# Sums of later tokens kept in float32 ahead of the up projection, products and transposes in a fixed order on TensorE, and a tile of its own for C11

## The chip, the cores and the metric

The kernel runs on one core of a Trainium2 chip. The metric is the device time of one execution in microseconds, given as the median of several runs. The engines are named as in the profile: PE is TensorE's matmul, DVE is VectorE, ACT is ScalarE, POOL is GpSimd, and SP is SyncE, whose queue issues nearly all transfers.

## The reference

The reference is one layer of a hybrid decoder over 1024 tokens of width 1024. The change touches only the end of it, from the output projection of the merged mixers to the feed-forward part:

```python
x = x + merged @ w_out[l]
u = rms_norm(x, norm_mlp_g[l]) @ mlp_up[l]          # 1024 x 1024 @ 1024 x 4096
x = x + jnp.square(jax.nn.relu(u)) @ mlp_down[l]    # 1024 x 4096 @ 4096 x 1024
```

All arrays are float32.

## The kernel before

The whole kernel is written with a tile framework. Each engine runs its instructions in a fixed order, and a tile waits for the last readers of the buffer that it takes over. A buffer is named by a tag in a pool: two tiles with one tag share the buffer in turn. The order on each engine is set when the program is built, by a scheduler that takes the instructions in the order of the program and moves those forward that are ready. `tc.issue_after(ins)` pins the instructions that are written in its block behind `ins` on their engine.

Every float32 product is made of three matmuls of a split operand (`mm3`, lines 229 to 236): high by high (L233), high by low (L234), low by high (L235). The split of an operand is two instructions (`split`, lines 1364 to 1367): a cast on ACT (L1365, the high part) and a subtraction on POOL or DVE (L1366, the low part). Split weights stand in three buffers for high parts (`whi`) and three for low parts (`wlo`).

The last part of the kernel is the function `tail` (line 1279). It works in these stages:

- **The output projection**, for the first 512 tokens (hf 0) and then for the later 512 (hf 1), each in two halves of the columns (n). It accumulates in four PSUM banks at a time, adds the residual on DVE (L1358) and normalises each tile of 128 tokens (`norm_tile`, L1314; its last instruction is L1319 on DVE). For n = 1 the banks are two of tag `g` and two of tag `w`. The transposes of the normalised tiles (`transposed`, tiles `nt_f`) also use the two banks of tag `w`.
- **The operands of the up projection.** `mlp_up` is multiplied in 8 groups of 512 columns. Each group is a 2 by 2 block product in Winograd's form with seven products. The activations are split by features and tokens into B11 and B21 (first tokens, features below and above 512), B12 and B22 (later tokens). The seven operands are B11, B21, B22, and T1 = B12 - B11, T2 = B22 - T1, T3 = B12 - B22, T4 = B21 - T2. `first_half` makes B11 and B21 between matmuls of the output projection. `second_half(j)`, for j from 0 to 3, makes slice j of the other operands: it transposes slice j and slice 4 + j of the later tokens into two banks (`p12`, `p22`), forms the sums with scale and subtraction on DVE (L1476, L1477, L1479), and at once splits each of them into its high and low part. The sums live in a tile `tt` that alternates between the buffers of tags `l4` and `l5`.
- **The groups.** `up_a(g)` makes the products with B11 (bank tile `ux`, called X) and B21 (bank tile `uy`), copies X into the group's block C11 (L1400 on ACT), adds Y to it (L1413) and squares its positive part (L1418). `up_b(g)` makes the other five products with T2, T1, T3, B22 and T4, of which T2, T3 and T4 accumulate on top of X, forms the remaining blocks and sums of them, and stores seven blocks to DRAM for the down projection. The first products of groups 0 and 1 are placed between the calls of `second_half`.

All outputs of a group lie in three tiles `uo` of tags `l4`, `l5` and `r1`. C11 is the first half of the tile of tag `l4`, and the copy into it is written in the function `outputs` (lines 1396 to 1400). So the copy for group g + 1 has to wait until group g is done with the whole tile of tag `l4`. T2's product accumulates on X, so it has to wait for that copy. The weights of a group come by `up_raw(g)` in two loads of 1 MB. For groups 0 and 1 these are written behind the output projection; the first of group 1 goes to tag `l3`, which held the residual tiles `x2` of the last 256 tokens.

## Time and profile before

| what | value |
|---|---|
| median of 3 runs | 2004.56 us (2002.54 to 2006.52) |
| the profiled execution's own time | 2009.52 us |
| its span, first to last instruction | 2007.7 us |
| mean granted clock of PE over the span | 0.981 |
| PE busy | 1928.6 us, 96% |
| PE weight load busy | 1533.4 us, 76% |
| DVE busy | 1147.2 us, 57% |
| ACT busy | 719.9 us, 36% |
| POOL busy | 737.7 us, 37% |

The profiled execution is one run. Its span is 1.8 us shorter than its own time, and its own time is 5.0 us above the median. Busy time is a share of the whole span, so it averages stages with different limits. A row of the timeline gives the start in microseconds, the duration, the engine, the line, the operation with its output and inputs, and in brackets the idle time ahead of it and what ended that. Matmuls overlap on PE, so the distance between two starts tells what one costs. The names of the profile leave out most numbers: `ux` is X of any group, `nt_f` any transposed bank.

### The profile page before, as it was taken

What the parts mean: (1) busy time and instruction counts of PE and PEld (TensorE: products, weight loads), DVE (VectorE), ACT (ScalarE), POOL (GpSimd) and SP (SyncE); (2) the same over time, 40 slices, a digit from 0 to 9 for tenths busy, and PEclk for the clock granted to TensorE, in tenths of its full rate; (3) what the DMA queues carried; (4) which work ended last, traced back from release to release, by engine and by line L of the source; (5) the groups of instructions that cost most, each with busy time, mean ns of one, the idle gap of its engine ahead of it and who ended that gap; (6) DMA issues with size and microseconds to landing.
All of it is one profiled execution on the core that took longest, in us unless ns stands there. A gap on an engine that the chain in (4) does not pass through costs nothing. (4 is left out here: it accounts for less than half of the span.)

```text
span 2007.7 us, 29664 instructions
## 1 busy us (share of the span) xinstructions
PE 1928.6 (96%) x11754; PEld 1533.4 (76%) x11754; DVE 1147.2 (57%) x1874; ACT 719.9 (36%) x1194; POOL 737.7 (37%) x596
## 2 busy tenths in 40 slices
PE   8999999999999999899999999997899999999999
PEld 6776677787677778677777778886788888788887
DVE  5555456656666564333333254248567667988875
ACT  5675223233333322333333222255232323333332
POOL 1343533343343341212262332335243444444443
PEclk9999999999999999999999999998999999999999
DMA  4122312221221221633353333533334449544231
GB/s 145 53 70 71 93 44 62 63 62 51 51 60 52 62 54 45 205 101 122 111 184 96 112 110 93 200 127 115 131 141 158 147 147 364 187 162 168 105 119 70
DMA packets 186529, 226.56 MB, mean 113 GB/s; under 512 B 38057, under 2 KB 132422, under 8 KB 186391
## 3 DMA queue, kind: packets, MB, share of 16 engines
q1 hardware_dynamic: 186214, 224.65, 34.0%
q8 instruction: 92, 1.51, 0.3%
q14 instruction: 47, 0.38, 0.1%
q0 software_dynamic: 160, 0.02, 0.0%
q10 hardware_dynamic: 16, 0.00, 0.0%
HBM read 162.89 MB, written 64.10 MB: 113 GB/s over the span
## 5 line engine op out<-in xcount | busy, mean ns | idle before, releaser
L233 PE MATMUL g_zg<-hh,wh_zg 128*128 128x512 f32 x384 | 155.1, 404 | 0.0
L235 PE MATMUL g_zg<-hh,wl_zg 128*128 128x512 f32 x384 | 152.3, 397 | 0.0
L234 PE MATMUL g_zg<-hl,wh_zg 128*128 128x512 f32 x384 | 152.3, 397 | 0.0
L1366 POOL TENSOR_TENSOR wl_d<-dr,wh_d 128x1024 fp32r<-128x1024 f32 x40 | 102.5, 2562 | 129.1 <-ACT wh_d L1365 120.7
L1366 DVE TENSOR_TENSOR du<-dq,du 128x1024 fp32r<-128x1024 f32 x56 | 125.5, 2242 | 21.8 <-ACT du L1365 21.2
L226 POOL TENSOR_TENSOR wl_zg<-wr_zg,wh_zg 128x1024 fp32r<-128x1024 f32 x24 | 57.5, 2396 | 163.7 <-ACT wh_zg L225 148.8
L235 PE MATMUL dx<-wh_d,du 128*128 128x512 f32 x256 | 99.8, 390 | 2.7 <-DVE du L1366 2.7
L233 PE MATMUL dx<-wh_d,du 128*128 128x512 f32 x256 | 99.6, 389 | 0.0
L234 PE MATMUL dx<-wl_d,du 128*128 128x512 f32 x256 | 99.6, 389 | 0.0
L1365 ACT CAST wh_d<-dr 128x1024 fp32r<-128x1024 f32 x40 | 42.1, 1052 | 144.8 <-PE dx L235 79.0
L233 PEld LDWEIGHTS g_zg<-hh,wh_zg 128*128 128x128 f32 x384 | 72.8, 190 | 17.9 <-issue 3.6
L235 PEld LDWEIGHTS g_zg<-hh,wl_zg 128*128 128x128 f32 x384 | 72.6, 189 | 16.4 <-issue 1.5
L234 PEld LDWEIGHTS g_zg<-hl,wh_zg 128*128 128x128 f32 x384 | 72.8, 190 | 15.7 <-issue 1.8
L1366 POOL TENSOR_TENSOR wl_a<-ur,wh_a 128x1024 fp32r<-128x1024 f32 x16 | 51.0, 3189 | 83.8 <-ACT wh_a L1365 83.8
L234 PE MATMUL g_z<-hl,wh_z 128*128 128x512 f32 x192 | 77.6, 404 | 0.0
L235 PE MATMUL g_z<-hh,wl_z 128*128 128x512 f32 x192 | 77.2, 402 | 0.0
L233 PE MATMUL g_z<-hh,wh_z 128*128 128x512 f32 x192 | 76.7, 399 | 0.4 <-DVE zsq L428 0.4
L773 DVE TENSOR_SCALAR s<-ac,wc 64x64 f32<-64x64 f32 x128 | 36.0, 282 | 68.3 <-PE ac L769 65.9
L1366 POOL TENSOR_TENSOR wl_s<-ur,wh_s 128x1024 fp32r<-128x1024 f32 x16 | 42.2, 2635 | 83.7 <-ACT wh_s L1365 83.4
L226 POOL TENSOR_TENSOR wl_wo<-wr_wo,wh_wo 128x1024 fp32r<-128x1024 f32 x16 | 38.5, 2412 | 79.3 <-ACT wh_wo L225 79.3
L1232 DVE SCALAR_TENSOR_TENSOR th<-th,pj 128x512 f32<-128x512 f32 x32 | 21.7, 683 | 72.7 <-PE pj L235 69.7
L1033 ACT ACTIVATE lg<-lg,nm 128x128 f32<-128x128 f32 (+1 forms) x96 | 42.2, 441 | 56.7 <-DVE nm L1031 56.7
(667 smaller groups left out, 5729.0 us busy)
## 6 DMA issues: line engine op xcount, KB each, us to landing
dq<-u_d SPq DMA_DIRECT2D x56, 512.0 KB
ur<-in_mlp_up_dram SPq DMA_DIRECT2D x16, 1024.0 KB
dr<-in_mlp_down_dram SPq DMA_DIRECT2D x16, 1024.0 KB
wr_zg<-in_w_in_dram SPq DMA_DIRECT2D x24, 512.0 KB
mg_d<-th SPq DMA_DIRECT2D x32, 256.0 KB
tb<-mg_d SPq DMA_DIRECT2D x32, 256.0 KB
wr_wo<-in_w_out_dram SPq DMA_DIRECT2D x16, 512.0 KB
wr_z<-in_w_in_dram SPq DMA_DIRECT2D x12, 512.0 KB
```

Source lines behind the costliest of these rows:

```text
L226: E.tensor_tensor(lo, raw, hi, ALU.subtract)
L233: PE.matmul(ps, lh, rh, start=first and i == 0, stop=False, skip_group_check=skip)
L234: PE.matmul(ps, lh, rl, start=False, stop=False, skip_group_check=skip)
L235: end = PE.matmul(ps, ll, rh, start=False, stop=last and i == n - 1, skip_group_check=skip)
L773: V.tensor_scalar(ns[half[h], :], pb[h][half[h], 128 * j + 64 * c : 128 * j + 64 * c + 64], wc[half[h], 2 * i + c : 2 * i + c + 1], None, ...
L1033: A.activation(lg[:, q, los[q] : 256], lg[:, q, los[q] : 256], AF.Exp, bias=nm[:, q : q + 1], accum_out=stat[:, 1, h, 2 * sp + q : 2 * sp ...
L1232: V.scalar_tensor_tensor(th, th, 1.0, ps, ALU.add, ALU.mult)
L1365: A.copy(hi, src)
L1366: E.tensor_tensor(lo, src, hi, ALU.subtract)
```

## The change

The change is confined to `tail` and to a pad in the caller that gives 320 bytes of each partition to the new tile. It does these things:

- Slices of the later tokens' sums are kept in float32 in four whole tiles, `f1`, `f2`, `f3` and `b22`, and are split afterwards in two halves of 1024 columns (`splits`), T2 first, then T1, T3, B22 and T4. The low parts of T2 and T1 are made on DVE, those of T3 on POOL, those of B22 and T4 on one of each.
- The first products and the transposes are pinned in a fixed order on PE (`st["pe"]`, `st["tr"]`): whole products between whole groups of transposes.
- C11 of each group goes to a tile of tag `u1` (`copy_p1`), and the block `u1` takes its old place in the tile of tag `l4`.
- The first half of group 1's first weights comes by a load of its own, `ur1a` of 512 KB, into the buffer of tag `u1`. The weights of group 0 are requested at the beginning of hf 1.
- The sums of group 0's weights (`sums(0)`) are made in between, and the low part of the weights `s1` of group 0 is made on POOL.
- In the output projection, n = 1 uses the banks `ac0` and `ac1` in place of the two of tag `w`. The transposes of `first_half` are placed in two calls of four slices.
- T3, T4 and B22 change buffers (tags `l6`, `l7`, `r7`, `l2`), and the small tiles of the norm move to the right-hand pool.

```diff
@@ tail @@
-                    pg.tile([P, 512], F32, tag="g", name=f"wo{hf}{n}{i}") if i < 2 else psum("w", 2, f"wo{hf}{n}{i}") for i in range(4)]
+                    pg.tile([P, 512], F32, tag="g", name=f"wo{hf}{n}{i}") if i < 2 else psum(f"ac{i - 2}", 1, f"wo{hf}{n}{i}") for i in range(4)]
...
-                    if hf == 1 and n == 0 and q > 0:
-                        first_half(range(3 * q - 3, min(3 * q, 8)))
+                    if hf == 1 and n == 0 and q in (1, 2):
+                        first_half(range(4 * q - 4, 4 * q))
...
+        def copy_p1(g):
+            c11 = st[g]["c11"] = lp.tile([P, 2, H], F32, tag="u1", name=f"c11{g}")
+            for m in range(2):
+                A.copy(c11[:, m, :], st[g]["X"][m])
+            return c11
...
+            if g == 1:
+                with tc.issue_after(st["f"].ins):
+                    w = wsplit(st[g]["a11"], V, f"a11{g}")
+            else:
+                w = wsplit(st[g][0][:, :, 0:256], G, f"a11{g}")
             for m in range(2):
-                up_product(g, w, "B11", X, True, (m,))
+                with tc.issue_after(st["pe"].ins) if "pe" in st else nullcontext():
+                    up_product(g, w, "B11", X, True, (m,))
                 yield
...
-            def outputs():
-                uo = [blk(t, [P, 2, 2, H], f"uo{g}{t}") for t in ("l4", "l5", "r1")]
-                st[g]["u"] = [uo[i // 2][:, i % 2] for i in range(6)]
-                for m in range(2):
-                    A.copy(st[g]["u"][0][:, m, :], X[m])
...
+            uo = [blk(t, [P, 2, 2, H], f"uo{g}{t}") for t in ("l4", "l5", "r1")]
+            a11 = st[g]["c11"]
+            u1, a12, a21, a22, s1, s2 = (uo[i // 2][:, i % 2] for i in range(6))
...
-            t = blk(f"l{4 + j % 2}", [P, 4, H], f"tt{j}")
-            b22, t1, t2, t3 = (t[:, i, :] for i in range(4))
-            h, l = B["B22"]
-            A.activation(b22, p22, AF.Copy, scale=g1)
-            V.scalar_tensor_tensor(t1, p12, g0, b11[:, j, :], ALU.mult, ALU.subtract)
-            V.scalar_tensor_tensor(t2, p22, g1, t1, ALU.mult, ALU.subtract)
-            A.activation(h[:, j, :], p22, AF.Copy, scale=g1)
-            V.scalar_tensor_tensor(t3, p12, g0, b22, ALU.mult, ALU.subtract)
-            V.scalar_tensor_tensor(l[:, j, :], p22, g1, h[:, j, :], ALU.mult, ALU.subtract)
-            for nm, x, E in (("T2", t2, G), ("T1", t1, V), ("T3", t3, G)):
-                split(x, B[nm][0][:, j, :], B[nm][1][:, j, :], E)
-            V.tensor_tensor(b21[:, j, :], b21[:, j, :], t2, ALU.subtract)
+            A.activation(b22[:, j, :], p22, AF.Copy, scale=g1)
+            f = V.scalar_tensor_tensor(f1[:, j, :], p12, g0, b11[:, j, :], ALU.mult, ALU.subtract)
+            st.setdefault("f", f)
+            V.scalar_tensor_tensor(f2[:, j, :], p22, g1, f1[:, j, :], ALU.mult, ALU.subtract)
+            V.scalar_tensor_tensor(f3[:, j, :], p12, g0, b22[:, j, :], ALU.mult, ALU.subtract)
...
+        for j, g in enumerate((0, 0, 1, 1)):
+            if j == 0:
+                next(steps[0])
+                next(steps[0])
+            next(steps[g])
+            second_half(j)
+            st["pe"] = st["tr"]
+            if j == 1:
+                sums(0)
+        two = [slice(0, 2), slice(2, 4)]
...
+        splits("T2", f2, ("r5", "r6"), (V, V))
+        st["pin"] = split.last
+        with tc.issue_after(split.last.ins):
+            splits("T1", f1, ("l1", "r4"), (V, V))
+            for _ in steps[0]:
+                pass
+            for c in two:
+                V.tensor_tensor(b21[:, c], b21[:, c], f2[:, c], ALU.subtract)
+            splits("T3", f3, ("l6", "l7"), (G, G))
+            splits("B22", b22, ("l12", "l0"), (G, V))
+            splits("T4", b21, ("r7", "l2"), (G, V))
```

**On PE, where the transposes of the later tokens begin.** `uy01` is the second bank of group 0's product with B21, `nt_f10` and `nt_f14` are the banks of slice 0. Before:

```order
L235 MATMUL uy00_12351<-B21h_11895,wl_a120_12348 128x512
L233 MATMUL uy01_12352<-B21h_11895,wh_a120_12347 128x512
L234 MATMUL uy01_12352<-B21l_11896,wh_a120_12347 128x512
L1329 MATMUL nt_f10_12323<-cg_92,xn2_11575 128x128
L1329 MATMUL nt_f14_12328<-cg_92,xn2_11575 128x128
L235 MATMUL uy01_12352<-B21h_11895,wl_a120_12348 128x512
L233 MATMUL uy01_12352<-B21h_11895,wh_a120_12347 128x512
L1329 MATMUL nt_f10_12323<-cg_92,xn2_11575 128x128
L1329 MATMUL nt_f14_12328<-cg_92,xn2_11575 128x128
```

and with the change:

```order
L235 MATMUL uy00_12320<-B21h_11896,wl_a120_12317 128x512
L1328 MATMUL nt_f10_12334<-cg_92,xn2_11572 128x128
L1328 MATMUL nt_f14_12339<-cg_92,xn2_11572 128x128
L1328 MATMUL nt_f10_12334<-cg_92,xn2_11572 128x128
L1328 MATMUL nt_f14_12339<-cg_92,xn2_11572 128x128
L1328 MATMUL nt_f10_12334<-cg_92,xn3_11573 128x128
L1328 MATMUL nt_f14_12339<-cg_92,xn3_11573 128x128
L1328 MATMUL nt_f10_12334<-cg_92,xn3_11573 128x128
L1328 MATMUL nt_f14_12339<-cg_92,xn3_11573 128x128
L233 MATMUL uy01_12321<-B21h_11896,wh_a120_12316 128x512
```

The eight transposes of a slice now stand together behind the whole of `uy00`, and `uy01` comes as a whole behind them. The three other slices follow in the same way behind `uy01`, `ux10` and `ux11`, and T2's product of group 0 follows the last.

**On DVE, the sums of the later tokens.** `tt0` and `tt1` hold the sums of slices 0 and 1, and `wl_s10` is the low part of group 0's weights `s1`. Before:

```order
L1479 SCALAR_TENSOR_TENSOR tt0_12333<-nt_f10_12323,par_100,tt0_12333 128x512
L1483 TENSOR_TENSOR b21_11898<-b21_11898,tt0_12333 128x512
L1476 SCALAR_TENSOR_TENSOR tt1_12375<-nt_f11_12365,par_100,b11_11897 128x512
L1366 TENSOR_TENSOR wl_s10_12540<-s10_12504,wh_s10_12539 128x1024
L1366 TENSOR_TENSOR T1l_12282<-tt0_12333,T1h_12281 128x512
L1480 SCALAR_TENSOR_TENSOR B22l_12280<-nt_f14_12328,par_100,B22h_12279 128x512
L1366 TENSOR_TENSOR T1l_12282<-tt1_12375,T1h_12281 128x512
L1477 SCALAR_TENSOR_TENSOR tt1_12375<-nt_f15_12370,par_100,tt1_12375 128x512
L1479 SCALAR_TENSOR_TENSOR tt1_12375<-nt_f11_12365,par_100,tt1_12375 128x512
L1483 TENSOR_TENSOR b21_11898<-b21_11898,tt1_12375 128x512
```

and with the change, where `wl_a111` is the low part of the weights of group 1's first product:

```order
L1374 TENSOR_TENSOR wl_a111_12385<-ur1a_12284,wh_a111_12384 128x1024
L1488 SCALAR_TENSOR_TENSOR f2_12280<-nt_f14_12339,par_100,f1_12281 128x512
L1489 SCALAR_TENSOR_TENSOR f3_12282<-nt_f10_12334,par_100,b22_12283 128x512
L1486 SCALAR_TENSOR_TENSOR f1_12281<-nt_f11_12360,par_100,b11_11898 128x512
L1488 SCALAR_TENSOR_TENSOR f2_12280<-nt_f15_12365,par_100,f1_12281 128x512
L1489 SCALAR_TENSOR_TENSOR f3_12282<-nt_f11_12360,par_100,b22_12283 128x512
L1486 SCALAR_TENSOR_TENSOR f1_12281<-nt_f12_12400,par_100,b11_11898 128x512
L1374 TENSOR_TENSOR T2l_12441<-f2_12280,T2h_12440 128x1024
L1488 SCALAR_TENSOR_TENSOR f2_12280<-nt_f16_12405,par_100,f1_12281 128x512
L1489 SCALAR_TENSOR_TENSOR f3_12282<-nt_f12_12400,par_100,b22_12283 128x512
L1486 SCALAR_TENSOR_TENSOR f1_12281<-nt_f13_12426,par_100,b11_11898 128x512
L1488 SCALAR_TENSOR_TENSOR f2_12280<-nt_f17_12431,par_100,f1_12281 128x512
```

The low parts of T1 and B22 and the subtraction from `b21` no longer stand between the sums of one slice and the next. The sum `f3` of a slice is the last reader of its first bank. The low part of T2 now stands on DVE, once between the sums of slice 2, and once behind those of slice 3.

**On DVE, where group 0 ends and group 1 begins.** `uo0l4`, `uo0l5` and `uo0r1` are the tiles of group 0's outputs. Before, the last readers of the tile that holds C11 are these:

```order
L1454 TENSOR_TENSOR uo0r1_12497<-uo0r1_12497,uo0l4_12495 128x1024
L1456 TENSOR_TENSOR uo0l5_12496<-uo0l5_12496,uo0l4_12495 128x1024
L1437 TENSOR_TENSOR ur20_12676<-ur20_12676 128x4x256
L1366 TENSOR_TENSOR wl_s11_12755<-s11_12719,wh_s11_12754 128x1024
L1460 TENSOR_TENSOR uo0l4_12495<-uo0l4_12495 128x1024
L1426 TENSOR_TENSOR s22_12965<-s12_12964,ur20_12676 128x1024
L1462 TENSOR_TENSOR uo0l5_12496<-uo0l4_12495,uo0r1_12497 128x1024
L1413 TENSOR_TENSOR uo1l4_12710<-uy10_12684,uo1l4_12710 128x512
```

and with the change the last readers of `c110` stand two and three rows behind the sum `uo0r1`:

```order
L1462 TENSOR_TENSOR uo0l5_12484<-uz01_12517,uo0l4_12483 128x512
L1456 TENSOR_TENSOR ur11_12481<-ur11_12481,s21_12694 128x4x256
L1424 SCALAR_TENSOR_TENSOR uo0l5_12484<-uo0l5_12484 128x1024
L1466 TENSOR_TENSOR uo0r1_12485<-uo0l5_12484 128x1024
L1429 TENSOR_TENSOR s12_12938<-ur20_12649,ur21_12651 128x1024
L1468 TENSOR_TENSOR uo0r1_12485<-uo0r1_12485,c110_12452 128x1024
L1470 TENSOR_TENSOR uo0l5_12484<-uo0l5_12484,c110_12452 128x1024
L1451 TENSOR_TENSOR ur20_12649<-ur20_12649 128x4x256
L1374 TENSOR_TENSOR wl_s11_12728<-s11_12693,wh_s11_12727 128x1024
L1474 TENSOR_TENSOR uo0l4_12483<-uo0l4_12483 128x1024
L1419 TENSOR_TENSOR c111_12683<-uy10_12657,c111_12683 128x512
```

Behind the second reader of `c110` nothing of group 0 holds the copy of C11 of group 1. The difference `ur11` and the sum `s12` for later weights stand ahead of those readers.

## Rows read from the trace of the kernel before

**Rows 1.** The page's head: the span, and PE's busy time.

```profile
span 2007.7 us, 29664 instructions
...
PE 1928.6 (96%) x11754; PEld 1533.4 (76%) x11754; DVE 1147.2 (57%) x1874; ACT 719.9 (36%) x1194; POOL 737.7 (37%) x596
```

**Rows 2.** Waits of PE, 1262 to 1560 us: total us, times, longest.

```profile
PE ux L233 <- ACT uo1l L1400: 6.4, 1, 6.4
PE nt_f L1329 <- DVE tt L1479: 4.8, 2, 2.5
PE ux L233 <- ACT uo0l L1400: 2.9, 1, 2.9
```

**Rows 3.** Timeline of PE: start, us, instruction, idle time before it.

```profile
1294.35 1.07 PE L233 MATMUL wo<-wh_wo,mh 128*128 128x512 f32 x4
1295.26 0.39 PE L234 MATMUL wo<-wl_wo,mh 128*128 128x512 f32 x1
...
1343.28 1.03 PE L1329 MATMUL nt_f<-cg,xn 128*128 128x128 f32 x8
...
1346.49 0.39 PE L234 MATMUL wo<-wl_wo,mh 128*128 128x512 f32 x1
...
1371.40 0.48 PE L235 MATMUL uy<-B21h,wl_a 128*128 128x512 f32 x1
...
1396.14 0.80 PE L233 MATMUL ux<-T2h,wh_s 128*128 128x512 f32 x1 [2.92 <-ACT uo0l L1400]
...
1399.20 0.40 PE L234 MATMUL ux<-T2l,wh_s 128*128 128x512 f32 x1
...
1430.04 0.39 PE L235 MATMUL uy<-B21h,wl_a 128*128 128x512 f32 x1
...
1439.98 0.44 PE L234 MATMUL ux<-T2l,wh_s 128*128 128x512 f32 x1
...
1514.40 0.39 PE L235 MATMUL uy<-B21h,wl_a 128*128 128x512 f32 x1
1515.99 0.50 PE L233 MATMUL ux<-T2h,wh_s 128*128 128x512 f32 x1 [1.20 <-ACT uo3l L1400]
1516.33 0.39 PE L234 MATMUL ux<-T2l,wh_s 128*128 128x512 f32 x1
```

**Rows 4.** Windows: busy us of PE, PEld, DVE, ACT, POOL; granted clock, DMA share, GB/s.

```profile
1280.00:1290.00 10.00, 10.00 (x46) 8.29 (x45) 2.77 (x4) 1.78 (x2) 3.95 (x2) 1.00 0.95 376
...
1390.00:1395.00 5.00, 2.17 (x8) 1.43 (x8) 4.12 (x7) 3.87 (x8) 3.44 (x3) 0.50 0.30 69
```

**Rows 5.** Timeline of DVE.

```profile
1367.21 0.75 DVE L1319 TENSOR_SCALAR xn<-x,rs_f 128x1024 f32<-128x1024 f32 x1
...
1376.92 0.75 DVE L1476 SCALAR_TENSOR_TENSOR tt<-nt_f,par,b 128x512 f32<-128x512 f32 x1 [2.48 <-PE nt_f L1329]
...
1427.08 1.21 DVE L1456 TENSOR_TENSOR uo0l<-uo0l,uo0l 128x1024 f32<-128x1024 f32 x1
...
1431.62 3.36 DVE L1426 TENSOR_TENSOR s<-s,ur 128x1024 f32<-128x1024 f32 x1
...
1434.90 1.21 DVE L1462 TENSOR_TENSOR uo0l<-uo0l,uo0r 128x1024 f32<-128x1024 f32 x1
```

**Rows 6.** Timeline of POOL.

```profile
1290.40 4.74 POOL L226 TENSOR_TENSOR wl_wo<-wr_wo,wh_wo 128x1024 fp32r<-128x1024 f32 x2 [6.12 <-ACT wh_wo L225]
...
1376.87 2.40 POOL L1366 TENSOR_TENSOR wl_s<-s,wh_s 128x1024 fp32r<-128x1024 f32 x1
...
1431.41 2.48 POOL L1366 TENSOR_TENSOR wl_s<-ur,wh_s 128x1024 fp32r<-128x1024 f32 x1 [7.62 <-ACT wh_s L1365]
```

**Rows 7.** Timeline of ACT.

```profile
1373.41 1.05 ACT L1365 CAST wh_a<-ur 128x1024 fp32r<-128x1024 f32 x1 [1.04 <-DMA ur<-in_mlp_up_dram]
...
1382.43 1.05 ACT L1365 CAST wh_s<-ur 128x1024 fp32r<-128x1024 f32 x1 [3.42 <-PE ux L234]
...
1436.19 1.07 ACT L1400 COPY uo1l<-ux 128x512 f32<-128x512 f32 x2 [4.85 <-DVE uo0l L1462]
```

More of the change, by code (lines that the diff above doesn't have):

```diff
@@ L372, in hybrid_block @@
           for hf in range(2) for x in range(2) for q in range(2)}
-    mhp.tile([P, 248], F32, name="pad1")
+    mhp.tile([P, 168], F32, name="pad1")
     mhi, mlo = ([[mt[(x, hf, k // 4)][:, k % 4, :] for hf in range(2)] for k in range(KT)] for x in range(2))
@@ L1338, in first_half, with up_raw @@
                 A.activation((b11 if k < 4 else b21)[:, j, :], ps, AF.Copy, scale=g)
+        st = {}
+        def up_raw(g, qs=(0, 1)):
+            for q in qs:
+                r = blk((("r2", "r3"), ("l3", "r0"))[g % 2][q], [P, 4, H], f"ur{g}{q}")
+                S.dma_start(r, io["mlp_up"][0][H * q : H * q + H, H * g : H * g + H].rearrange("(k p) c -> p k c", p=P))
+                st.setdefault(g, {})[q] = r
         for hf in range(2):
             if hf == 1:
+                up_raw(0)
                 operand("B11", "l8", "l9")
@@ L1365, in split @@
             A.copy(hi, src)
-            E.tensor_tensor(lo, src, hi, ALU.subtract)
+            split.last = E.tensor_tensor(lo, src, hi, ALU.subtract)
             return hi, lo
@@ L1406, in up_a @@
             for m in range(2):
-                up_product(g, w, "B21", Y, True, (m,))
+                with tc.issue_after(st["pe"].ins) if "pe" in st else nullcontext():
+                    up_product(g, w, "B21", Y, True, (m,))
                 yield
             if g < 2:
-                outputs()
-            c11 = st[g]["u"][0]
-            for m in range(2):
-                V.tensor_tensor(c11[:, m, :], Y[m], c11[:, m, :], ALU.add)
-            relu2(c11)
+                c11 = copy_p1(g)
+            with tc.issue_after(st["pin"].ins) if g == 0 else nullcontext():
+                for m in range(2):
+                    V.tensor_tensor(c11[:, m, :], Y[m], c11[:, m, :], ALU.add)
+                relu2(c11)
             S.dma_start(u_d[g, 0], c11)
@@ L1463, in up_b @@
             S.dma_start(u_d[g, 2], a22)
-        for nm, th, tl in (("B22", "l12", "l0"), ("T1", "l1", "r4"), ("T2", "r5", "r6"), ("T3", "r7", "l2")):
-            operand(nm, th, tl)
+        f2, f1, f3, b22 = (blk(t, [P, 4, H], nm) for t, nm in (("l4", "f2"), ("l5", "f1"), ("r7", "f3"), ("l2", "b22")))
         def second_half(j):
@@ L1493, in tail @@
-        next(steps[0])
-        second_half(2)
-        next(steps[1])
-        second_half(3)
-        next(steps[1])
-        np_.__exit__(None, None, None)
-        operand("T4", "l6", "l7")
-        for j in range(4):
-            split(b21[:, j, :], B["T4"][0][:, j, :], B["T4"][1][:, j, :], V if j % 2 else G)
-        up_raw(1, (1,))
-        sm2_ = tc.tile_pool(name="u1p", bufs=1)
-        sm2 = sm2_.__enter__()
+            A.activation(b22[:, j, :], p22, AF.Copy, scale=g1)
+            f = V.scalar_tensor_tensor(f1[:, j, :], p12, g0, b11[:, j, :], ALU.mult, ALU.subtract)
@@ new lines, in second_half @@
+            st.setdefault("f", f)
+            V.scalar_tensor_tensor(f2[:, j, :], p22, g1, f1[:, j, :], ALU.mult, ALU.subtract)
+            V.scalar_tensor_tensor(f3[:, j, :], p12, g0, b22[:, j, :], ALU.mult, ALU.subtract)
+        r = lp.tile([P, 4, 256], F32, tag="u1", name="ur1a")
+        S.dma_start(r, io["mlp_up"][0][0:H, H : H + 256].rearrange("(k p) c -> p k c", p=P))
+        st[1] = dict(a11=r)
+        steps = {g: up_a(g) for g in range(8)}
+        for j, g in enumerate((0, 0, 1, 1)):
[7 more added lines that the diff above has]
+                sums(0)
@@ new lines, in tail, with splits @@
+        two = [slice(0, 2), slice(2, 4)]
+        def splits(nm, src, tags, engines):
+            operand(nm, *tags)
+            for c, E in zip(two, engines):
+                split(src[:, c], B[nm][0][:, c], B[nm][1][:, c], E)
+        splits("T2", f2, ("r5", "r6"), (V, V))
[9 more added lines that the diff above has]
+            splits("T4", b21, ("r7", "l2"), (G, V))
@@ L1505, in tail @@
+        up_raw(1)
         for g in range(8):
```

42 lines of the change are left out of this document (15 added, 27 removed).

## The prediction

> **What bounds the kernel now.** I read the page's head first: PE is busy for 1928.6 of 2007.7 us [rows 1], and the change takes no matmul away. So it can only give back time in which PE waits or runs at its lower clock. The waits of PE between 1262 and 1560 us come next. The longest is 6.4 us for the copy of group 1's C11, then come 4.8 us of transposes that wait for the sums `tt`, and 2.9 us for the copy of group 0's C11 [rows 2]. What such a place costs in all is read from PE's timeline as elapsed time less the work at full pace. Four matmuls take 0.91 us from start to start, 0.228 us each, and eight transposes take 1.03 us, 0.13 us each [rows 3].
>
> - A, the later tokens' operands: from 1371.40 to 1399.20 there are 27.8 us. In them PE starts 32 matmuls (1 of `uy`, 24 of `ux` of group 1, 7 of T2's product) and 24 transposes, 7.3 + 3.1 = 10.4 us of work. Lost: 17.4 us.
> - B, group 1's T2: from 1430.04 to 1439.98 there are 9.94 us with 8 matmuls, 1.8 us. Lost: 8.1 us.
> - C, the output projection: from 1343.28 to 1346.49 there are 3.21 us with 8 transposes and one matmul, 1.26 us. Lost: 1.95 us.
> - D, group 3's T2: from 1514.40 to 1516.33 there are 1.93 us with 2 matmuls, 0.46 us. Lost: 1.5 us.
>
> Together that is 29.0 us, all by [rows 3], and it is the most that the change can give. A and B hold more than their idle time because the granted clock falls: it is 0.50 in 1390 to 1395 us, the lower of the two levels (1.2 GHz), after PE had waited several times [rows 4]. Seven matmuls then take 3.06 us from 1396.14 to 1399.20, against 1.6 at full pace, so a fall costs about 1.5 us. After the shorter wait of 1.20 us at 1515.99 PE is back at its full pace with the second matmul [rows 3].
>
> **The change part by part.**
>
> *Banks.* In C PE waits since the third and fourth bank of n = 1 are still held by transposes. Now they are `ac0` and `ac1`, emptied two matmul groups earlier. The 1.95 us go, and no other bank is late.
>
> *The early loads.* `ur1a` now stands on SP's queue ahead of a load of `w_out`. 512 KB at the 376 GB/s of that time [rows 4] are 1.4 us. The weights behind it were cast from 1289.28 [rows 7], the first of the two low parts from 1290.40 was done about 2.4 us later [rows 6], and PE first takes that at 1295.26 [rows 3]: 2.5 us of slack cover it. Were that gone, a us late would be a us lost, once. Group 0's first weights (1 MB, 2.8 us at that rate) pass one load of `w_out`, with 24 matmuls (5.5 us) of an earlier tile as cover. In return the cast `wh_a` of group 1 no longer waits for its transfer [rows 7], which opens A.
>
> *Group 1's C11.* The copy started at 1436.19 [rows 7], when the last sum L1462 was done (from 1434.90). The readers that alone count now ended with L1456 at 1427.08 + 1.21 = 1428.3 [rows 5]. The copies take 1.07 us, and PE is done with the last `uy` at 1430.3: the wait would vanish. But the new order puts `ur11` and `s12` ahead of the readers. From the start of T4's product DVE has six instructions to the last reader, of 1.2 us, and one of 0.7 us. That is 7.9 us, or 10 to 12 if one or two are held by POOL. With the copy it is 9 to 13 us, while T4 and `uy` give PE 48 matmuls, 10.9 us. I take 0.7 us, with the ends 0 and 2.5. D goes in the same way: two sums of 1.2 us less are waited for there, against a wait of 1.20 us.
>
> *The operands.* I replay the new order with a sum at 0.75 us, a subtraction of 1024 columns at 1.21, a cast at 1.05, a POOL subtraction at 2.40 and a product of 12 matmuls at 2.73 [rows 3, 5 to 7], and let neighbours on one engine overlap by 0.1 us, an estimate. 0 is the start of the first transposes. The norm's last instruction started at 1367.21 [rows 5] and comes earlier now by about as much as the products do, so I let 0 wait for nothing.
>
> - `nt_f11` needs `f3` of slice 0. DVE does `f1`, the low part of `a111`, `f2`, `f3` from 1.15 to 4.4; PE is done with `uy01` at 3.8. Wait 0.7 (to 2.9 if `a111` is held by POOL).
> - `nt_f12` is in time. `nt_f13` needs `f3` of slice 2, behind the low part of T2's first half. POOL is on B22 from 8.3 to 10.7, so that part ends at 11.8 and `f3` at 13.2. PE is free at 12.1. Wait 1.3 (0 to 3.5).
> - T2's second half needs ACT. There a cast for `s3` waits for `ux11`, as at 1382.43 [rows 7], and five instructions follow it: the cast of T2 ends at 18.1, its low part at 19.2. PE has used up the first half at 17.1. Wait 1.7 (1.0 to 3.9).
> - T1's low parts share DVE and POOL with T3's second half and `s4`: ready at 22.7 and 26.2, where PE asks at 21.7 and 24.1. Wait 3.1 (0.7 to 5.3).
> - B22's second half, and the evacuation of X before T4 behind eight more instructions on DVE: wait 2.7 (0 to 5.6).
>
> These are 9.5 us in place of A's 17.4. With C11 it makes 10.2, with the ends 2.4 and 23.7. No single wait reaches 2 us by much, so I count no fall of the clock; three falls of 1.5 us are the upper end.
>
> *Held by POOL* means this: a sum of two SBUF tiles on DVE that began 0.2 us after a POOL subtraction took 3.36 us instead of 1.21, while a sum that reads a PSUM bank kept its 0.75 us though POOL was at work [rows 5, 6]. The price is 2.15 us each time. I put it on four instructions of the replay. The Trainium skill (SBUF — State Buffer, section "Who interferes with whom") says that a VectorE instruction with two inputs in SBUF and a GpSimd instruction that reads SBUF lock each other out for a whole instruction, and that the order of issue decides who waits. The rows agree with it; read at its strictest it makes the slow rival below.
>
> *At nothing:* the first readers of the down projection's accumulators come 96 matmuls behind its start (21.9 us), so the later release of `r7` and `l2` is hidden, as four loads of 512 KB are 5.6 us. Group 0's last store stands behind `ur30` on SP's queue; its buffer is wanted only by group 1's fourth product. Were either late, PE would wait for the rest of the transfer.
>
> **Sum.** 29.0 - 10.2 = 18.8 us less. The rows come from an execution of 2009.5 us, whose span is 2007.7; the median is 5.0 us lower. I take the difference from the median: 2004.6 - 18.8 = **1985.8 us**. The ends are 1978.0, with the short waits, and 2003.8, with the long ones and three falls of the clock.
>
> **Rivals.**
>
> - *All is hidden* (1978.0 us). For it: DVE and POOL have less to do in this stretch than before. Against it: the cast of T2's second half cannot come sooner, since ACT is held until `ux11` ends.
> - *The fixed order gives nothing in A* (29.0 - 17.4 = 11.6 less, 1993.0 us). For it: each bank is still freed by the third sum of its slice, PE can no longer fill the gap with parts of `uy01`, and the clock may fall again. Against it: three sums take 2.1 us, and 2.7 us of matmuls stand between two slices.
> - *C11's wait gets another name* (18.8 - 7.4 = 11.4 less, 1993.2 us). `s12` waits for group 2's second weights, whose buffer is freed by the last split of group 0. If they land late, the readers of `c110` stand behind `s12`. Against it: by the replay that split comes some 10 us ahead.
> - *DVE is locked out by POOL* (slower). Between `a111` and `ur11` DVE has 14 instructions with two SBUF inputs. If each is held, that is 14 x 2.15 = 30.1 us, and 3.0 of waits remain without: 33.1 - 29.0 = 4.1 us more, **2008.7 us**. This is the strict reading of the rule named above. It decides from 12 of the 14 on; the rows show one such hold, and POOL was idle for 7.62 us ahead of the subtraction that caused it [rows 6].
>
> **How the numbers follow.** The forecast has 0.65, all hidden 0.07, the order for nothing 0.14, C11 under another name 0.10, the lock 0.04. A measurement can tell about 0.2% (4 us) from no change. Only the lock reaches 2000.6 us or more, with a small tail of the two rivals at 1993: faster 0.93, same 0.04, slower 0.03. The range goes from 1979 to 1996 us: it leaves out most of the first rival, the lock and the upper tails.
>
> **What would show it.** Right: no wait for C11 of groups 1 and 3, no wait at C, and from the first transposes to T2's end several waits of 0.5 to 2 us with the clock at 1.00. Wrong in the order: waits of over 2 us ahead of `nt_f` and a clock of 0.50. Wrong in C11: a wait of T2's first matmul of group 1 on ACT. Wrong by the lock: DVE's T1, T2 and `b21` rows at 3 us or more. Time lost in the output projection or at the down projection's start would be a cause that I have priced at nothing.

## The result, and the profile after

The changed kernel takes 1980.26 us (median, 1979.13 to 1980.51); the kernel before, run beside it, takes 2005.54 (2002.54 to 2009.33). The ratio is 0.9872, 95% interval 0.9854 to 0.9890: about 25 us less, where 18.8 were forecast. The time lies inside the range, at its fast end.

The page's head, with PE's busy time down by 10 us for the same matmuls (compare [rows 1]):

```profile
span 1978.7 us, 29639 instructions
...
PE 1918.6 (97%) x11754; PEld 1528.5 (77%) x11754; DVE 1143.5 (58%) x1868; ACT 717.3 (36%) x1184; POOL 727.8 (37%) x590
```

Waits of PE from 1262 to 1560 us (total us, times, longest), against [rows 2]:

```profile
PE ux L233 <- ACT T2h L1373: 1.6, 1, 1.6
PE uz L233 <- DVE c L1419: 1.0, 1, 1.0
PE ux L233 <- ACT c L1391: 0.7, 1, 0.7
PE nt_f L1328 <- DVE f L1488: 0.5, 1, 0.5
PE ux L234 <- DVE T2l L1374: 0.5, 1, 0.5
```

No wait reaches 2 us. The waits on `uo1l`, `tt`, `uo0l` and `uo3l` are gone; what is left is split over five places. The same five in PE's timeline (start, us, instruction, idle time before it), against [rows 3]:

```profile
1373.42 1.31 PE L1328 MATMUL nt_f<-cg,xn 128*128 128x128 f32 x8 [0.53 <-DVE f L1488]
...
1379.07 0.74 PE L233 MATMUL ux<-T2h,wh_s 128*128 128x512 f32 x2 [1.56 <-ACT T2h L1373]
1380.33 0.79 PE L234 MATMUL ux<-T2l,wh_s 128*128 128x512 f32 x1 [0.52 <-DVE T2l L1374]
...
1385.37 0.50 PE L233 MATMUL uz<-T1h,wh_s 128*128 128x512 f32 x1 [1.03 <-DVE c L1419]
...
1413.56 0.50 PE L233 MATMUL ux<-T2h,wh_s 128*128 128x512 f32 x1 [0.70 <-ACT c L1391]
```

Windows of the changed kernel (busy us of PE, PEld, DVE, ACT, POOL; granted clock, DMA share, GB/s), against [rows 4]: there is still one fall of the clock to the lower level (0.50, 1.2 GHz), for 3 us behind the waits for T2; in the window from 1390 us it is full again (1.00).

```profile
1380.40:1383.40 3.00, 3.00 (x7) 2.41 (x8) 3.00 (x1) 0.00 (x0) 2.10 (x1) 0.50 0.64 246
1390.00:1395.00 5.00, 5.00 (x23) 4.13 (x22) 5.00 (x3) 3.78 (x6) 3.27 (x1) 1.00 0.00 0
```

**Where the time came from.** I cut the profiled executions at two places, the first matmul of the output projection and the first of the down projection, read from PE's timeline in each kernel. "Ahead" is the time to the first cut, and no edit here touches what it computes; "middle" lies between the cuts, "down" behind them.

| kernel | ahead | middle | down | median of the runs, us | ratio to before (95%) |
|---|---|---|---|---|---|
| before | 1264.4 | 431.2 | 312.0 | 2005.5 | 1 |
| changed | 1260.1 | 409.4 | 309.2 | 1980.3 | 0.9872 (0.9854–0.9890) |
| e1, C11 back | 1261.5 | 420.9 | 309.2 | 1990.4 | 0.9925 (0.9905–0.9944) |
| e2, order free | 1255.6 | 418.4 | 315.2 | 1990.1 | 0.9920 (0.9900–0.9940) |
| e3, swap in changed | 1255.0 | 409.5 | 308.4 | 1979.2 | 0.9869 (0.9847–0.9890) |
| e4, swap in before | 1254.0 | 434.2 | 310.2 | 2000.1 | 0.9980 (0.9966–0.9994) |
| e5, banks back | 1256.8 | 416.7 | 309.2 | 1984.1 | 0.9894 (0.9872–0.9916) |
| e6, order in before | 1260.1 | 426.3 | 312.0 | 1996.8 | 0.9960 (0.9946–0.9975) |
| e7, own bank | 1255.6 | 409.9 | 309.2 | 1979.1 | 0.9868 (0.9844–0.9892) |
| e8, T2 in singles | 1255.4 | 409.7 | 309.3 | 1978.7 | 0.9867 (0.9845–0.9890) |
| e9, no early load | 1259.7 | 413.9 | 309.3 | 1981.5 | 0.9886 (0.9865–0.9908) |
| e10, splits on DVE | 1259.0 | 408.7 | 309.2 | 1978.5 | 0.9863 (0.9847–0.9879) |
| e11, e7 + e8 + e10 | 1258.8 | 412.1 | 309.2 | 1982.2 | 0.9892 (0.9874–0.9909) |
| e12, T3 on DVE, singles | 1261.8 | 407.6 | 309.5 | 1976.8 | 0.9862 (0.9836–0.9888) |

So the change gives 21.8 us in the middle and 2.9 us in the down projection. The stretch ahead differs by up to 10 us between executions, with no edit that would explain it. The difference of two profiled spans (here 29.0) is therefore not the gain, and below I compare middles and downs.

A middle is one execution, and it has scatter of its own: e4, whose code is that of the kernel before up to the down projection, has 434.2 where that kernel has 431.2; e3 and the changed kernel, equal in the same way, agree within 0.1. A middle that differs by less than some 3 us is therefore a reading of its rows and not a measured gain, and the ratios decide where they can. Of the four parts taken out singly (e1, e2, e5, e9), e1 and e2 have intervals clear of the changed kernel's; those of e5 and e9 overlap it.

### The profile page after: what moved, and what is told of

It reads as the page before. It is cut to its first block, busy times and chain, and to the rows that moved or that the text cites. A ratio compares the mean times of both kernels' runs of the same rounds, so it can differ in the third digit from the quotient of the medians.

```text
span 1978.7 us, 29639 instructions
## 1 busy us (share of the span) xinstructions
PE 1918.6 (97%) x11754; PEld 1528.5 (77%) x11754; DVE 1143.5 (58%) x1868; ACT 717.3 (36%) x1184; POOL 727.8 (37%) x590
## 5 line engine op out<-in xcount | busy, mean ns | idle before, releaser
L1374 POOL TENSOR_TENSOR wl_a<-ur,wh_a 128x1024 fp32r<-128x1024 f32 x15 | 46.8, 3117 | 72.9 <-ACT wh_a L1373 72.9
L1232 DVE SCALAR_TENSOR_TENSOR th<-th,pj 128x512 f32<-128x512 f32 x32 | 21.8, 684 | 73.7 <-PE pj L235 71.3
```

Of the source, the lines that this page charges most:

```text
L1232: V.scalar_tensor_tensor(th, th, 1.0, ps, ALU.add, ALU.mult)
L1374: split.last = E.tensor_tensor(lo, src, hi, ALU.subtract)
```

## The experiments

P1, P2 and P4 are a group's products with B11, B21 and T1; their banks are `ux`, `uy` and `uz`.

**e1: C11 back in the group's first output tile, from group 1 on.**

```diff
-            c11 = st[g]["c11"] = lp.tile([P, 2, H], F32, tag="u1", name=f"c11{g}")
+            if g:
+                st[g]["uo"] = [blk(t, [P, 2, 2, H], f"uo{g}{t}") for t in ("l4", "l5", "r1")]
+                c11 = st[g]["c11"] = st[g]["uo"][0][:, 0]
+            else:
+                c11 = st[g]["c11"] = lp.tile([P, 2, H], F32, tag="u1", name=f"c11{g}")
...
+            if g:
+                u1 = lp.tile([P, 2, H], F32, tag="u1", name=f"u1{g}")
```

> The changed kernel with one part undone: from group 1 on C11 lies again in the group's first output tile (and P1 + P2 in the tile of its own), as before the change. Theory (the C11 part of the change is what removed the 8.1 us at group 1 and the 1.5 us at group 3): about 1.0 us of wait that the changed kernel still has at group 1 turns back into some 8, and group 3 loses 1.5 again: the profile's span becomes 8 to 9 us longer than the changed kernel's 1978.7, median about 1988 to 1990, with PE waiting for a copy or an add into uo1l between 1405 and 1425 us. Rival (the gain at group 1 came from the float32 sums leaving VectorE and GpSimd earlier, not from the tile): within 2 us of the changed kernel, no wait on uo1l above 2 us.

Its waits of PE in the same stretch:

```profile
PE ux L233 <- ACT uo1l L1395: 8.9, 1, 8.9
...
PE ux L233 <- ACT uo3l L1395: 1.3, 1, 1.3
```

The middle is 11.5 us longer: 8.9 + 1.3 us of waits come back where 0.7 us was, and behind the long one nine matmuls run at half pace, some 1.8 us. By its ratio the kernel is some 10.6 us slower than the changed one. The theory holds, the rival falls; with the other parts in place the tile is worth a little more than it cost before (8.1 + 1.5). Why isn't shown; VectorE's sums come in another order now.

**e2: the fixed order on PE taken out.**

```diff
-                with tc.issue_after(st["pe"].ins) if "pe" in st else nullcontext():
+                with nullcontext():
...
-            with tc.issue_after(st["pe"].ins):
-                up_product(g, w, "T2", X, False)
+            up_product(g, w, "T2", X, False)
```

(The first replacement is made for both products of `up_a`.)

> The changed kernel without the fixed order on PE: up_product in up_a and the T2 product are no longer pinned behind the last transpose; the float32 sums stay. Theory (float32 sums and late splits carry the gain at the later tokens' operands, the order is a help of a few us): PE's time between the first later-token transposes and the end of group 0 gets 0 to 4 us longer, median 1980 to 1985. Rival (the fixed order carries the larger part of those 17.4 us): 8 us or more longer, median 1988 or above, with a wait for the transposes' readers that grows.

```profile
PE ux L233 <- ACT T2h L1373: 5.0, 2, 4.3
PE ux L234 <- DVE T2l L1374: 2.4, 2, 1.8
PE nt_f L1328 <- DVE f L1487: 1.6, 1, 1.6
```

The middle is 9.0 us longer, which is the rival's number: without the pins the scheduler puts the first half of T2's product ahead of the last eight transposes, and PE stands there waiting for T2's operands. The down projection grows by 6.0 us as well, with one wait of 3.6 us for an accumulator, though no line of it was edited. VectorE's order at that place is the changed kernel's; but from the first sum of the down weights to the first addition into an accumulator GpSimd held five of its instructions, for some 9.6 us together (two instructions of group 7 took 3.31 and 2.11 us, three sums of the down weights 3.42, 3.41 and 3.42), where four were held for some 6.2 us in the changed kernel. By the ratios e2 is 9.6 us slower than the changed kernel and not 15, so a part of this may belong to the one execution.

**e6: the fixed order alone, in the kernel before.** The transposes' last instruction is kept in a list, and `up_product` in `up_a` (twice) and for T2 is put under the same pin; nothing else.

> The kernel before with the fixed order alone: the first products and the T2 product are pinned behind the transposes of the step ahead of them; sums and splits stay as they were, quarter by quarter. Theory (the order lets the transposes of each quarter come 1 to 3 us sooner, but VectorE and GpSimd still have all of a quarter's splits between two sums, so the transposes wait for them as before): 0 to 5 us less than the kernel before at the later tokens' operands, ratio 0.998 to 1.000. Rival (the order is the main thing, the float32 sums a detail): 8 us or more less, ratio under 0.996.

```profile
PE ux L233 <- ACT uo1l L1403: 5.1, 1, 5.1
PE nt_f L1331 <- DVE B22l L1486: 5.0, 2, 4.0
PE nt_f L1331 <- DVE tt L1485: 1.9, 1, 1.9
```

The middle is 4.9 us shorter, the top of what the theory allowed; a fall of the clock behind the wait at C (0.50 from 1343 to 1346 us), which the kernel before did not have, costs it some 1.5 us. The ratio says more: 0.9960, 8 us less with 5 to 11 in the interval, which is outside the theory's 0.998 and at the rival's edge. The transposes' waits stay (5.0 + 1.9 us), only their names change. So the order is good for 5 to 8 us with the old sums and some 9 with the new ones: not a detail, and not the whole of A. That the rest of A comes from sums that free the banks earlier is argued and not shown, since no run takes the float32 sums out, or puts them in, by themselves.

**e5: the later columns' banks back to those of the transposes.**

```diff
-  ... else psum(f"ac{i - 2}", 1, f"wo{hf}{n}{i}") for i in range(4)]
+  ... else psum("w", 2, f"wo{hf}{n}{i}") for i in range(4)]
```

> The changed kernel with the projection's second banks put back: tiles 2 and 3 of the later columns take the transposes' two banks again, not the ac banks. Theory (the banks were what removed the 1.95 us wait of the projection): the wait of PE for the readers of the first half's transposes comes back, 1.5 to 2.5 us longer from the projection's start to the first product for up than the changed kernel, nothing else moves; median about 1982. Rival (the wait went because the transposes are made in two batches of four, after the first two weight quarters): under 0.5 us longer.

Waits of PE, and the window behind the first of them:

```profile
PE uz L233 <- DVE c L1419: 2.5, 1, 2.5
PE wo L233 <- ACT b L1337: 1.8, 1, 1.8
...
PE nt_f L1328 <- DVE xn L1318: 1.4, 2, 0.8
```

```profile
1340.00:1343.00 3.00, 3.00 (x8) 2.33 (x8) 0.00 (x0) 0.00 (x0) 0.00 (x0) 0.50 0.00 0
```

The wait at C comes back at its old size, but the middle is 7.3 us longer, not 2 (by the ratios some 4 us, with intervals that overlap). Cut at the same matmuls in both kernels, it says where: 3.7 us in the projection, the wait and the half pace behind it; 2.1 at two transposes that now wait for the norm's last rows; 1.5 behind T1's first matmul. The rows of PE from T2's second half to there, and the window behind T1's wait:

```profile
1381.53 0.73 PE L233 MATMUL ux<-T2h,wh_s 128*128 128x512 f32 x2 [1.60 <-ACT T2h L1373]
1382.79 0.50 PE L234 MATMUL ux<-T2l,wh_s 128*128 128x512 f32 x1 [0.53 <-DVE T2l L1374]
...
1387.86 0.80 PE L233 MATMUL uz<-T1h,wh_s 128*128 128x512 f32 x1 [2.49 <-DVE c L1419]
```

```profile
1388.00:1391.00 3.00, 3.00 (x7) 2.35 (x8) 3.00 (x3) 0.39 (x1) 1.44 (x1) 0.50 0.00 0
```

The waits for T2 are those of the changed kernel, but here the clock falls behind T1's wait and not behind T2's. From T2's second half to T1's first matmul it takes 6.33 us, and 6.30 in the changed kernel (from 1379.07 to 1385.37): VectorE sets that time, and the fall inside it cost nothing, since PE only waited less at its end. A wait that looks like 2 us can carry a fall of the clock and the order of a later stage with it.

**e9: no early load of group 1's first weights.**

```diff
-        r = lp.tile([P, 4, 256], F32, tag="u1", name="ur1a")
-        S.dma_start(r, io["mlp_up"][0][0:H, H : H + 256].rearrange("(k p) c -> p k c", p=P))
-        st[1] = dict(a11=r)
+        up_raw(1, (0,))
```

(The split of group 1's first weights then reads the first columns of that whole tile, and only the second tile is loaded behind.)

> The changed kernel without the early copy of group 1's first weights: no ur1a in the tile of its own; group 1's first tile of weights is loaded whole at that place into the tile that the kernel before used. Theory (the early load is no gain by itself, since the fixed order alone decides when those weights are needed, and the tile before comes free early enough): the same as the changed kernel within 1 us from the projection's start to the down projection (409.4). Rival (the tile becomes free only after the later tokens' rows are stored, so the weights land late, as the 2.6 us wait for the first weight split in the kernel before shows): 2 to 5 us longer.

```profile
PE uz L233 <- DVE c L1419: 2.5, 1, 2.5
PE ux L233 <- ACT wh_a L1373: 2.4, 1, 2.4
```

The middle is 4.5 us longer, which is the rival's number; by the ratios it is some 3 us, with intervals that overlap. The 2.4 us for the cast `wh_a` is the wait that opened A before, and a fall of the clock follows it (0.50 from 1370 to 1372 us).

**e3 and e4: two buffers' tags exchanged at the down projection's start.** It gained 2.9 us, and the prediction had it at nothing. In the kernel before, PE waits three times there for a split of `u` (total, times, longest):

```profile
PE dx L235 <- DVE du L1366: 2.7, 3, 1.1
```

The same edit was made in the changed kernel (e3) and in the kernel before (e4):

```diff
-        for q, t in enumerate(("r7", "l2", "l12", "l0")):
+        for q, t in enumerate(("l6", "l2", "l12", "l0")):
...
-        uring, uraw = ("r5", "r6", "l1", "r4"), ("l10", "l11", "l6")
+        uring, uraw = ("r5", "r6", "l1", "r4"), ("l10", "l11", "r7")
```

> The changed kernel, where only two tags of the down projection are exchanged: the first accumulator tile takes l6 and the third buffer for u takes r7 (in the changed kernel T4's high part lies in r7, T3's in l6). No matmul, split or sum is touched. Theory (the 2.8 us that the down projection's start gained, and that the prediction had at nothing, came from the third buffer of u: before it lay where T4 was, the last operand that group 7 reads, and now lies where T3 was): the three waits of PE for du come back at the start of the down projection, 2 to 4 us together, median 1982 to 1984, span about 2.8 us over 1978.7. Rival (the start gained because VectorE came out of group 7 with less work behind it): no change, within 0.6 us of 1978.7 in the span and no wait for du.

> The kernel before, with the same two tags exchanged and nothing else: the third buffer of u takes r7 (where T3 lies there), the first accumulator tile l6 (where T4 lies). Theory (the buffer's tag alone makes the gain at the down projection's start): the three waits for du (0.61, 0.95, 1.15 us) go, 2 to 3.5 us less than the kernel before, ratio about 0.9985. Rival (it is group 7's backlog on VectorE): waits and span as before within 0.6 us, ratio 1.000.

e4 wins 1.8 us in the down projection and two of the three waits for `du` go; its ratio says 4 us, with 1 to 7 in the interval. e3 loses nothing: no wait for `du` appears, and the down projection is 0.8 us shorter. So the tag can help the kernel before, but it isn't what the change gained. The timelines of VectorE show the difference. First the kernel before, then the changed one (the first sum of the down weights, and the split that PE waited for):

```profile
1700.22 1.21 DVE L1584 TENSOR_TENSOR dt0l<-dr 128x1024 f32<-128x1024 f32 x1
...
1717.36 1.22 DVE L1366 TENSOR_TENSOR du<-dq,du 128x1024 fp32r<-128x1024 f32 x1
```

```profile
1658.63 1.22 DVE L1602 TENSOR_TENSOR dt0l<-dr 128x1024 f32<-128x1024 f32 x1 [0.23 <-PE ux L234]
...
1679.07 2.57 DVE L1374 TENSOR_TENSOR du<-dq,du 128x1024 fp32r<-128x1024 f32 x1 [0.79 <-ACT du L1373]
```

The down projection starts at 1695.65 and 1669.54. Before, the first sum comes 4.6 us after that, behind most of group 7's last sums, and the split 21.7 us after. In e4 the sum stands where it stood (4.6 us after) and the exchange of tags alone brings the split forward to 15.8 us after. In the changed kernel the sum comes 10.9 us ahead of the start and the split 9.5 behind it (in e3 18.5, still in time). VectorE had no idle time in the kernel before from 1691 us on, so a split that stands later in its order is later on PE. Which edit made the scheduler put the sums there is open: e1, e5 and e9 keep 309 us, and in e2, without the pins, the first sum still stands 8.4 us ahead of the start.

**e7 and e8: P4 in banks of its own; then T2's second half split quarter by quarter as well.** These try to remove what is left.

```diff
-            Y = [pg.tile([P, 512], F32, tag="g", name=f"uz{g}{m}") for m in range(2)]
+            Y = [pg.tile([P, 512], F32, tag="g", name=f"uz{g}{m}") if g else psum("w", 2, f"uz{g}{m}") for m in range(2)]
```

```diff
-            for c, E in zip(two, engines):
+            for c, E in zip(two if len(engines) == 2 else [slice(0, 2), slice(2, 3), slice(3, 4)], engines):
...
-        splits("T2", f2, ("r5", "r6"), (V, V))
+        splits("T2", f2, ("r5", "r6"), (V, V, V))
```

> The changed kernel, where group 0's P4 product (the one with T1) takes the transposes' two banks, which nobody uses any more at that place, in place of the banks that P2's result still fills. Theory (the 1.0 us that T1's first matmul waits for the add that reads P2 is that bank): this wait goes, 1 to 1.5 us less from first product to the down projection than the changed kernel's 316.0. Rival (T1's low parts, which come after each other on VectorE, are late too and take the wait over): within 0.4 us of 316.0, with a wait for T1l in its place.

> As the run with the bank of its own, and the split of T2's second half made in two pieces, the third quarter by itself and then the fourth, so that the third does not wait for the fourth's sum. Theory (PE's 1.6 us for T2's high part and 0.5 us for its low part are the time that ScalarE and VectorE need for two quarters at once after the last sum): 1.5 to 3 us less than with the bank alone, and with it the clock fall of about 1.5 us that follows. Rival (two more instructions on ScalarE and VectorE in the same place cost what the earlier start gives): within 0.5 us of the run with the bank alone.

Neither shortens the middle (409.9 and 409.7). In e7 the wait for the add goes, and 0.7 us for T1's low part and 1.9 us for a copy take its place. In e8 the wait for T2's high part goes, and T1's low part holds PE for 2.1 us. By the time both rivals hold (e7 is 0.5 us longer, where its rival allowed 0.4); but in e8 the time doesn't go to the two added instructions. VectorE and GpSimd show why:

```profile
1375.64 6.70 DVE L1374 TENSOR_TENSOR T1l<-f,T1h 128x1024 fp32r<-128x1024 f32 x2
```

```profile
1372.75 5.20 POOL L1374 TENSOR_TENSOR T3l<-f,T3h 128x1024 fp32r<-128x1024 f32 x2
1377.95 3.31 POOL L1374 TENSOR_TENSOR wl_s<-ur,wh_s 128x1024 fp32r<-128x1024 f32 x1
```

Three subtractions stand back to back on GpSimd, and the two on VectorE take 6.70 us.

**e10: the low parts of T3, B22 and T4 on VectorE.**

```diff
-            splits("T3", f3, ("l6", "l7"), (G, G))
-            splits("B22", b22, ("l12", "l0"), (G, V))
-            splits("T4", b21, ("r7", "l2"), (G, V))
+            splits("T3", f3, ("l6", "l7"), (V, V))
+            splits("B22", b22, ("l12", "l0"), (V, V))
+            splits("T4", b21, ("r7", "l2"), (V, V))
```

> The changed kernel, with the low parts of T3, B22 and T4 all on VectorE; GpSimd keeps the weight splits only. Theory (VectorE is late for T1's low part and for the add that frees P2's bank because GpSimd's low part of T3 holds it up: two T1l took 4.52 us where two alone would take 2.4): T1l's two go to some 2.4 us, the 1.0 us wait for the add goes, 1 to 2 us less than 316.0 from first product to down projection. Rival (four more low parts, 4.8 us of work, make VectorE late for T3, B22 or T4): a new wait of 1 us or more for one of these, same time or longer.

The same pair of T1, first in the changed kernel (with the GpSimd row beside it), then in e10, where GpSimd is idle from 1375.11 to 1381.86:

```profile
1380.19 4.52 DVE L1374 TENSOR_TENSOR T1l<-f,T1h 128x1024 fp32r<-128x1024 f32 x2
...
1380.05 2.45 POOL L1374 TENSOR_TENSOR T3l<-f,T3h 128x1024 fp32r<-128x1024 f32 x1 [1.46 <-ACT T3h L1373]
```

```profile
1378.17 2.35 DVE L1374 TENSOR_TENSOR T1l<-f,T1h 128x1024 fp32r<-128x1024 f32 x2
```

2.35, 4.52 and 6.70 us for the same two instructions: the steps are 2.17 and 2.18 us, and a GpSimd subtraction took 2.40 to 2.45. The Trainium skill (SBUF — State Buffer, section "Who interferes with whom") says that a VectorE instruction with two inputs in SBUF and a GpSimd instruction that reads SBUF contend; the three rows agree with it. PE's rows from T2's second half to T1, in e10:

```profile
1377.05 0.73 PE L233 MATMUL ux<-T2h,wh_s 128*128 128x512 f32 x2 [1.66 <-ACT T2h L1373]
1378.31 0.50 PE L234 MATMUL ux<-T2l,wh_s 128*128 128x512 f32 x1 [0.53 <-DVE T2l L1374]
...
1381.18 0.50 PE L233 MATMUL uz<-T1h,wh_s 128*128 128x512 f32 x1 [0.31 <-DVE c L1419]
```

That stretch takes 4.13 us where the changed kernel takes 6.30: the 2.17 us by which the pair is shorter. The waits for T2 are the same and the clock stays at 1.00 behind them. The wait for the add falls from 1.0 to 0.3 us. But the middle falls by 0.7 only, since later waits (1.3 us for a sum of group 0, 0.5 more at C11) come in.

**e11 and e12: both kinds together.** e11 has the edits of e7, e8 and e10; e12 that of e8 without the bank, and only T3 on VectorE.

> Bank of its own for P4, T2's second half split in two, and the low parts of T3, B22 and T4 on VectorE, together. Theory (the three limits stand one behind the other: T2's two-quarter split, the bank, and T1l that GpSimd holds up; each alone only uncovers the next, as T1l at 6.70 us in the run before showed, so all three must go): the waits there fall from 1.6 + 0.5 + 1.0 us and a clock fall to under 1.5 us, 2.5 to 4.5 us less than 316.0. Rival (VectorE is now simply full between the last sum and T4): within 1 us of 316.0, with the wait at T3, B22 or T4.

> The changed kernel with T2's second half split in two, and only T3's two low parts moved from GpSimd to VectorE; P4 keeps its banks, B22 and T4 keep their engines. Theory (the run with all of it made VectorE late at group 1's C11 and the weight split, because four more low parts and the early P4 came at once; with two more low parts behind T1's, T2's wait and the clock fall go and nothing new appears): 2 to 4 us less than 316.0 from first product to down projection, median about 1977. Rival (any low part more on VectorE comes back at group 1's C11): within 1 us of 316.0 or longer, with a wait for c of 2 us or more.

Waits of PE from the projection to the end of group 7, first e11, then e12:

```profile
PE ux L233 <- ACT c L1391: 4.0, 1, 4.0
PE uy L235 <- POOL wl_a L1374: 1.9, 1, 1.9
PE ux L233 <- ACT uo0l L1445: 0.9, 1, 0.9
```

```profile
PE ux L233 <- ACT c L1391: 1.9, 1, 1.9
PE uz L233 <- DVE c L1419: 1.7, 1, 1.7
PE nt_f L1328 <- DVE f L1488: 0.5, 1, 0.5
```

In e11 all of the waits for T2, T1 and the bank are gone, and the middle is 2.6 us longer: the waits stand at group 1 now. Neither forecast had that number; the cause is the rival's, a step later than it was put: VectorE's queue is longer by what it took over, and the readers of group 0's C11 stand at its end. e12 is the best middle of all, 407.6, but 1.8 us shorter instead of the 2 to 4 expected: T2's waits and the clock's fall are gone, and 1.7 us at the bank and 1.9 at C11 stand in their place. Its ratio overlaps the changed kernel's, so that it is the faster is a reading of the profile, not of the times.

## Why the prediction was right, and by how much off

**The ceiling** of 29.0 us was right: by the same subtraction on the changed kernel 7.2 us are left between 1255 and 1485 us, and 29.0 - 7.2 = 21.8 is what the middle gained. With the middle of e4 in place of before's it would be 24.8, so how near the forecast came is in part luck.

**The waits left** were put at 10.2 us and are 7.2, term by term:

| term | forecast | measured |
|---|---|---|
| `nt_f11` | 0.7 | 0 |
| `nt_f13` | 1.3 | 0.7 |
| T2's second half | 1.7 | 2.5 |
| T1's low parts | 3.1 | 2.7: 1.2 of waiting for P2's bank, and 1.5 of half pace ahead of it |
| B22's second half, X before T4 | 2.7 | 0 |
| C11 of group 1 | 0.7 | 1.0 |

These make 6.9; the rest is spread over gaps too small to name. (By its own figures the replay's first two waits are 0.6 and 1.1 us, 0.3 less in all; nothing hangs on that.) The early loads cost nothing: no matmul of the output projection waits in the changed kernel. The cast that the slack of 2.5 us was counted from is this row of the kernel before:

```profile
1289.28 1.05 ACT L225 CAST wh_wo<-wr_wo 128x1024 fp32r<-128x1024 f32 x1 [7.46 <-DMA wr_wo<-in_w_out_dram]
```

The replay had the casts right. It let T2's last one end at 18.1 us, and counted from the first later-token transposes (1361.67) it ends at 17.4. This is ACT's row:

```profile
1372.71 1.05 ACT L1373 CAST wh_s<-ur 128x1024 fp32r<-128x1024 f32 x1 [1.82 <-PE ux L234]
...
1377.97 1.05 ACT L1373 CAST T2h<-f 128x1024 fp32r<-128x1024 f32 x1
```

The cast for `s3` holds ACT until PE frees its buffer, and five instructions follow, as written. The two early waits were over-sized, and so PE reached this place sooner and waited longer.

**"T1's low parts ... wait 3.1"** was near in size and right in its mechanism. The low parts were done at 1384.7, 23.0 us after the start, against 22.7 and 26.2 in the replay: the pair was held by one GpSimd subtraction, not two. The instruction that PE waited for is the add that empties P2's bank; it stands behind the two low parts on VectorE (1384.64), and the replay had no row for it. But the hold sets when it comes: without it, in e10, T1's first matmul comes 2.17 us sooner behind T2's second half.

**"I count no fall of the clock"** failed: the clock was at 0.50 behind T2's waits of 1.56 and 0.52 us, neither of which reaches 2 us. It did no harm there, because VectorE sets the time of T1's first matmul (6.30 us with the fall, 6.33 in e5 without). That it fell at a harmless place is luck: in e5, e6 and e9 a fall costs about 1.5 us.

**"B22's second half, and the evacuation of X before T4 ... wait 2.7"** is the step that was most over-sized: 2.7 us against nothing. No matmul waited there: behind 5 us of T1's product and as much of the next, VectorE caught up. The holds that were to make it late are four in VectorE's rows from T2's first low part to T4's, at 2.28, 4.52, 4.10 and 3.43 us, the number that was forecast. No matmul of B22, T3 or T4 waits for them; but VectorE has no idle time from 1379 us to the end of C11's last reader at 1412.9, so each of them also puts off that reader, and with it the wait that is left there.

**"At nothing: the first readers of the down projection's accumulators"** was misread, and the price of the whole start was wrong by 2.9 us. Some 21.9 us behind the start PE needs the first readers done; they themselves began 15.8 us behind it in the kernel before (1711.45) and 12.0 in the changed one (1681.57). No load held them there, but PE waits 0.5 us for one of them, and 3.6 in e2. The step looked at two buffers' release and not at the order of VectorE, which the change moved there too.

Waits that were 3.0 us shorter than forecast, most of them at B22 and X, and 2.9 us of the down projection make the distance between 18.8 and the 24.7 of the two stretches.

**The rivals.** That all is hidden falls by 7.2 us. That the order gives nothing falls by e2 and e6. That C11's wait gets another name is half true: 1.0 us is left, and it is the last reader of the one tile (L1470 on VectorE), not `s12`. The lock's mechanism is in the rows of e5, e8 and e10, but from `a111` to `ur11` six instructions are held, for some 9.4 us together, and not fourteen for 30.1.

**The parts** taken out singly from the changed kernel cost 11.5 (tile), 9.0 (order), 7.3 (banks) and 4.5 us (early load), 32.3 in all by the middles, more than the 21.8 that the whole gives there. By the ratios they cost some 10.6, 9.6, 4.4 and 2.8 us, 27.4 against 25.7, which is not clear of the noise. The rows of e5 and e9 show how the parts overlap: a wait taken out at one place changes the wait at the next. So no share of the gain belongs to one part alone, and the float32 sums have no run of their own.

## What to carry to other kernels

Replay the order of each engine in turn and include the instructions that free a bank, not those alone that make an operand: one wait that stayed was on an add that the replay left out. When several engines are close to full in a stretch, taking one wait away uncovers the next; price the wait that will stand in its place before counting a gain (e7, e8, e11). A stretch that another engine sets doesn't need the full clock on PE: from T2's second half to T1 it took 6.30 us with a fall and 6.33 without. And compare like stretches: cut both traces at the same instruction.

## What the hardware showed that I had not expected

- The stretch ahead of the output projection took from 1254.0 to 1264.4 us in the fourteen profiled executions, 10 us that no edit explains. It is more than most parts are worth.
- The same wait of 1.85 us at the same place (C) was followed by a granted clock of 1.00 in the kernel before and of 0.50 in e5 and e6. The same waits for T2, 1.6 and 0.5 us, were followed by 0.50 in the changed kernel and by 1.00 in e5 and e10. In the row below, from the kernel before, PE starts 15 matmuls in 3 us, where e5 started 8:

```profile
1346.50:1349.50 3.00, 3.00 (x15) 2.46 (x14) 0.00 (x0) 0.27 (x1) 0.00 (x0) 1.00 0.03 5
```

  What decides it isn't settled here.
- A square that reads one tile twice on VectorE (L1424, 128x1024) is held by GpSimd like a sum of two: 3.43 us in the changed kernel with GpSimd at work, 1.21 in e10 without.

```profile
1392.13 3.43 DVE L1424 SCALAR_TENSOR_TENSOR c<-c 128x1024 f32<-128x1024 f32 x1
```
